# Squares of the gated output, summed step by step in a hybrid decoder layer on one core

## The chip, the core and the metric

The kernel runs on one core of one Trainium2 chip. The metric is the device time of one launch in microseconds (us), as the median of several runs. An engine's name here is that of the profile: PE is TensorE, DVE is VectorE, ACT is ScalarE, POOL is GpSimd, SP is SyncE.

## The reference

One layer over 1024 positions and 1024 channels, in float32. A projection of the normed and modulated input feeds a gated spatial mixer and a Mamba-2 state-space mixer; both go through a projection, are gated, added, projected and added to the input. What the change touches is the end of the state-space mixer: its output `y` of 2048 channels is gated by `silu(z)` and normed by groups of 256 channels.

```python
y_b = ssd_scan(xh, dt, a, bm, cm)                      # chunks of 128 positions
y_b = y_b + xh * d_skip[:, None]
yz = (y_b.reshape(b, s, 2048) * jax.nn.silu(ssm_z)).reshape(b, s, 8, 256)
y_b = rms_norm(yz, ssm_norm_w.reshape(8, -1)).reshape(b, s, 2048)   # yz * rsqrt(mean(yz * yz) + 1e-6) * w
merged = jax.nn.sigmoid(g_a) * (y_a @ w_proj_a) + jax.nn.sigmoid(g_b) * (y_b @ w_proj_b)
```

So for each of 8 groups and each of 1024 positions one sum of 256 squares is needed, and from it one factor.

## The kernel before

The kernel has four parts in time. First the input is normed and transposed. Then, to about 920 us, TensorE multiplies the wide input projection in pairs of 128 columns; other work is hung beside it as tasks. Then comes the **state-space stage**, from about 920 to 1150 us. Last come the products with `w_proj_b` in units named p1, p5, p2, p3, p6, p7 and p4 of eight each, and the output products.

The state-space stage has 32 steps: 8 groups times 4 slices of 256 positions (two chunks of 128). The list `order` runs two groups side by side, so that steps n and n+2 are neighbours of one group. Each step has these parts, for step n:

- `fetch`: SyncE loads `dcy`, the decay row of the step broadcast to all partitions, and then `sl`, the slice with B, C, x and silu(z). There are five buffers of each; the loads stand in SyncE's queue in program order (`pin`), and a load waits until the buffer's last reader is done. For `sl` that is the gating multiply of five steps before.
- `decay`: ACT takes two `ea` (L999) from `dcy`, POOL masks `dcy` in place (L1002), ACT takes eight exponentials of it (L1007).
- `prep`: TensorE makes the products `pc` and transposes `pc` and `px`; DVE makes `xd` and `xe` and multiplies `dcy` (L1027); ACT copies `bn`.
- `front`: TensorE makes `yi` and the state's additions `sp`; POOL and DVE carry the state `st` (L1055, L1057).
- `back`: TensorE makes `yn` from the states. `evacuate` follows: DVE writes `y1` from `yi` and the skip (L1083) and `ym` from `yn` and `ea` (L1087), POOL adds them into `y1` (L1088) and multiplies by the gate into `yz` (L1089). `y1` and `ym` have two buffers each; `yz` holds two steps.

After every second step of a group (`post`), ACT stores `yz`. TensorE's program order is fixed by `pin`: front of step n, some products `pma` of the other branch's projection as filling (`draw`), back of step n, prep of step n+2. Front, back and prep count as one slot each. `later(k, f)` runs f after k more slots. All instructions that are not pinned are put into each engine's queue by a planner that follows expected ready times; on the chip each queue then runs in that order, and an instruction that waits holds up those behind it on its engine.

The sums of squares: five slots after `post`, ACT squares `yz` in place (L1108, it must wait until the store has read it), and POOL adds the two channel halves (L1109). Seventeen slots after `post`, TensorE sums over the partitions with four one-column products per 512 positions (`pq`, the squares as the standing operand), DVE scales them into `ssq` (L1117), positions on partitions, and once per group POOL takes the power −0.5 (L1121). Eight slots on, TensorE transposes the factors (`pr`), DVE copies them (L1131), and ACT stores them to `rs_d`. For the second half of the last two groups the squares go to tiles of their own (L1104), and sums, power and transpose come at the units k = 1, 4 and 6 of p1. The units after the stage load `rs_d` as a broadcast (`rb`) and norm `yz` with it (`y_norm`, L1416).

## Time and profile before

| | us |
|---|---|
| median of 3 runs | 1405.37 |
| lowest and highest run | 1405.05 and 1412.27 |
| the profiled execution: time | 1407.67 |
| the profiled execution: span from first to last instruction | 1405.9 |
| PE busy in the span | 1377.1 (98%) |
| DVE, ACT, POOL busy | 1062.4, 797.0, 213.0 |
| mean granted clock of PE | 0.997 of full |

Times in the profile are microseconds from the span's start. In the timeline a row is: start, length, engine, line, operation, output from inputs, and in brackets how long the engine had been idle and what released it. SPq and ACTq are DMA issues. In a table by windows the figure behind the busy times is the granted clock. In a list of waits a row has the sum, the number and the longest. A matmul in float32 shows as two records.

### The profile page before, as it was taken

How to read it: one execution, taken by the hardware profiler on the slowest of the kernel's cores; microseconds unless marked ns; L12 is line 12 of the kernel's file. 1: busy time of each engine (PE TensorE's matmuls, PEld its weight loads, DVE VectorE, ACT ScalarE, POOL GpSimd, SP SyncE). 2: the span in 40 equal slices, each digit the busy share in tenths (PEclk: the TensorE clock that was granted, in tenths of full speed). 3: DMA queues.
4: the chain of work that ended last, by engine and by line, in shares of the span. 5: the costliest groups of instructions: out<-in, count | busy, mean ns of one | idle time of the engine just before them, and what ended most of it. 6: DMA issues, size and time to landing. Idle time of an engine off the chain costs nothing.

```text
span 1405.9 us, 20633 instructions
## 1 busy us (share of the span) xinstructions
PE 1377.1 (98%) x7035; PEld 1139.9 (81%) x7035; DVE 1062.4 (76%) x1863; ACT 797.0 (57%) x1471; POOL 213.0 (15%) x208
## 2 busy tenths in 40 slices
PE   8999999999999999999999999999999999999997
PEld 6688888888888888888887888888888877878886
DVE  4786776777778889889788796388667767876976
ACT  5764576556656665556565555677766723322443
POOL 0000000000000011111000010038778740000001
PEclk9999999999999999999999999999999999999999
DMA  8653343343344777787675774598778749878903
GB/s 263 173 165 98 113 120 105 105 121 120 116 125 134 214 202 239 236 248 232 192 221 156 240 214 135 173 353 318 262 253 296 275 168 328 320 231 296 350 33 120
DMA packets 273150, 283.37 MB, mean 202 GB/s; under 512 B 15341, under 2 KB 223637, under 8 KB 273045
## 3 DMA queue, kind: packets, MB, share of 16 engines
q1 hardware_dynamic: 185684, 198.52, 44.4%
q10 hardware_dynamic: 87360, 83.54, 17.8%
q8 instruction: 55, 0.90, 0.3%
q14 instruction: 51, 0.41, 0.1%
HBM read 194.55 MB, written 87.46 MB: 201 GB/s over the span
## 4 chain that ended last, share of the span: by engine, by line
PE 80%; DMA 8%; DVE 5%; POOL 2%; issue 2%; ACT 1%; SPq 1%; ACTq 0%; DVEq 0%; POOLq 0%
PE xcb L574 6%; PE xuz L574 6%; PE xz L574 6%; PE xx L574 5%; PE xg L574 5%; PE x L1477 4%; PE yp L1477 4%; PE ox L1676 3%; PE yuz L574 3%; PE ycb L574 3%; PE pma L81 3%; PE xv L574 3%; PE yz L574 3%; PE yg L574 3%; PE yx L574 3%; DMA dcy<-acs_d 3%
## 5 line engine op out<-in xcount | busy, mean ns | idle before, releaser
L793 POOL TENSOR_TENSOR wog<-wog,gb 128x256 f32<-128x256 f32 x16 | 18.3, 1159 | 676.6 <-PE zz L574 413.3
L1007 ACT ACTIVATE dcy<-dcy,nacs 128x128 f32<-128x128 f32 x256 | 78.6, 388 | 14.9 <-POOL dcy L1002 14.5
L1002 POOL TENSOR_SCALAR_AFFINE_SELECT dcy<-dcy 128x1024 f32<-128x1024 f32 x32 | 35.0, 1095 | 135.7 <-ACT ea L999 132.3
L999 ACT ACTIVATE ea<-dcy 64x512 f32<-64x512 f32 x64 | 40.1, 626 | 14.2 <-DMA dcy<-acs_d 13.8
L920 ACT ACTIVATE ac<-ac 128x1024 f32<-128x1024 f32 x32 | 33.9, 1060 | 23.0 <-DVE ac L918 22.8
L81 PE MATMUL pma<-yh,wah 128*128 128x512 f32 x128 | 43.3, 419 | 0.0
L1027 DVE TENSOR_TENSOR dcy<-dcy,pc 128x1024 f32<-128x1024 f32 x32 | 39.0, 1218 | 4.8 <-PE pc L84 3.0
L81 PE MATMUL pma<-yh,wal 128*128 128x512 f32 x128 | 42.5, 413 | 0.0
L1089 POOL TENSOR_TENSOR yz<-y,sl 128x512 f32<-128x512 f32 x32 | 41.4, 1295 | 1.1
L1087 DVE TENSOR_TENSOR ym<-yn,ea 128x512 f32<-128x512 f32 (+1 forms) x32 | 19.9, 622 | 28.5 <-PE yn L81 28.3
L81 PE MATMUL pma<-yl,wah 128*128 128x512 f32 x128 | 40.1, 394 | 0.0
L1088 POOL TENSOR_TENSOR y<-y,ym 128x512 f32<-128x512 f32 (+1 forms) x32 | 36.6, 1144 | 14.4 <-DVE ym L1087 14.4
L81 PEld LDWEIGHTS yn<-sl,st 128*128 128x128 f32 x224 | 30.3, 190 | 8.3 <-issue 4.4
L81 PE MATMUL yn<-sl,st 128*128 128x128 f32 x224 | 31.6, 276 | 4.9 <-DVE st L1057 4.9
L1416 DVE SCALAR_TENSOR_TENSOR yn<-yn,par,rb 128x512 f32<-128x512 f32 x32 | 24.0, 749 | 15.7 <-DMA yn<-yb_d 15.5
L81 PE MATMUL sp<-xe,bn 128*128 128x256 f32 x112 | 32.6, 408 | 3.3 <-DVE ssq L1117 1.7
L81 PE MATMUL yi<-dcy,xd 128*64 128x128 f32 x512 | 35.7, 283 | 0.0
L918 DVE SCALAR_TENSOR_TENSOR ac<-c2x,cwt,ac 128x1023 f32<-128x1023 f32 (+2 forms) x24 | 31.2, 1300 | 5.3 <-ACT ac L916 5.1
L918 DVE SCALAR_TENSOR_TENSOR ac<-c2cb,cwt,ac 128x1023 f32<-128x1023 f32 (+2 forms) x24 | 31.1, 1296 | 4.4 <-ACT ac L916 4.3
L1691 POOL TENSOR_TENSOR r<-r,fnw 128x512 f32<-128x512 f32 x2 | 2.5, 1296 | 203.7 <-DMA out_dram<-r 203.7
L1055 POOL TENSOR_TENSOR st<-st,cd 128x256 f32<-128x256 f32 x48 | 32.1, 668 | 8.0 <-PE yn L81 5.3
L918 DVE SCALAR_TENSOR_TENSOR ac<-c1cb,cwt,ac 128x1023 f32<-128x1023 f32 (+2 forms) x24 | 31.6, 1318 | 1.3 <-ACT ac L916 1.3
(2980 smaller groups left out, 4390.9 us busy)
## 6 DMA issues: line engine op xcount, KB each, us to landing
sl<-s_d SPq DMA_DIRECT2D x32, 768.0 KB
s_d<-ac ACTq DMA_DIRECT2D x32, 512.0 KB
dcy<-acs_d SPq DMA_DIRECT2D x32, 512.0 KB
aw<-in_ada_w_dram SPq DMA_DIRECT2D x16, 512.0 KB
wbr<-in_w_proj_b_dram SPq DMA_DIRECT2D x64, 128.0 KB
wb_d<-wbb ACTq DMA_DIRECT2D x32, 256.0 KB
wb_d<-wbc ACTq DMA_DIRECT2D x32, 256.0 KB
yb_d<-yz ACTq DMA_DIRECT2D x32, 256.0 KB
```

The costliest lines, as they stand in the source:

```text
L81: pin(PE.matmul(acc, l, r, start=first, stop=last))
L574: pin(PE.matmul(ps, lw[:, k * P : (k + 1) * P], r[k], start=first and n + k == 0, stop=n == 2 and k == 3, skip_group_check=not first))
L918: V.scalar_tensor_tensor(ac[:, s:], cc[:, : S - s], conv_wt[:, 3 - s, i : i + 1], ac[:, s:], op0=ALU.mult, op1=ALU.add)
L920: A.activation(ac, ac, AF.Silu)
L999: A.activation(ea[hh * HD : (hh + 1) * HD], dcy.rearrange("p (j e) i l -> p e j (i l)", e=2)[hh * HD : (hh + 1) * HD, hh], AF.Exp)
L1002: G.affine_select(out=d8, in_=d8, compare_op=ALU.is_ge, fill=-1e30, base=0, pattern=[[0, 2 * HPG], [1, P]], channel_multiplier=-1)
L1007: A.activation(dcy[:, h, i, :], dcy[:, h, i, :], AF.Exp, bias=sub[:, i, h : h + 1])
L1027: V.tensor_tensor(d3, d3, pc[:, 0:256].unsqueeze(1).to_broadcast([P, HPG, 256]), op=ALU.mult)
L1088: G.tensor_add(y1[:, :, t0:], y1[:, :, t0:], m[:, :, t0:])
L1089: G.tensor_mul(yz, y1, sl[:, 4:6])
L1477: pin(PE.matmul(ps[j], a[:, v, js], r, start=first and n + k == 0, stop=n == 2 and k == KT - 1, skip_group_check=not first))
L1676: pin(PE.matmul(ps, a[:, tsl], b[:, cs], start=first and n + j == 0, stop=n == 2 and j == 3, skip_group_check=not first))
```

## The change

The squares of each step are taken by themselves. One slot after `evacuate`, ACT squares the step's `yz` into the tile `y1` that held y without its gate, whose content is no longer needed. Two slots later TensorE sums them over the partitions in the other way round: the ones are the standing operand, 32 columns wide, and the squares move, so that each block of 128 positions fills a strip of 32 partitions of the result. The two channel halves are added in PSUM, so POOL's add goes. DVE scales the two strips into a row tile (`cwt`, `tri` or `par`), and after every second step of a group ACT stores one row of each of the four strips to a new tile in memory, `ms_d`. Once per group SyncE loads it back with positions on partitions, POOL takes the power, and ACT stores the factors to `rs_d`; the transposes go. The last two groups do the same at units 1 to 7 after the stage, and their sums no longer come there.

```diff
@@ -55,6 +55,7 @@
 
     acs_d = dt_([NG, 4, HPG, 256], "acs_d")
     rs_d = [dt_([1, S], f"rs_d{g}") for g in range(NG)]
+    ms_d = [dt_([1, S], f"ms_d{g}") for g in range(NG)]
     v_d = dt_([NG, P, NCH * P], "v_d")
     ya_d = [dt_([P, S], f"ya_d{g}") for g in range(NG)]
     mt_d = [dt_([P, S], f"mt_d{g}") for g in range(NG)]
@@ -1087,52 +1088,51 @@
             V.tensor_tensor(m[:, :, t0:], yn.rearrange("p (j l) -> p j l", j=2)[:, :, t0:], ea[:, :, t0:], op=ALU.mult)
             G.tensor_add(y1[:, :, t0:], y1[:, :, t0:], m[:, :, t0:])
             G.tensor_mul(yz, y1, sl[:, 4:6])
+            later(1, self.square, s, yz, y1)
 
         def post(self, q):
 
             g = self.g
             for j in range(2):
                 store(yb_d[2 * g + j][:, q * 512 : (q + 1) * 512], self.yz[q][:, j])
-            yz = self.yz[q]
-            if g < NG - 2 or q == 0:
-                later(5, self.squares, yz, [yz[:, j] for j in range(2)])
-                later(17, self.post2, q, [yz[:, 0]])
-            else:
-                self.late = [turn(r, f"sq{g}", F32) for r in (y1_r, ym_r)]
-                with tc.high_priority():
-                    for j in range(2):
-                        A.activation(self.late[j], yz[:, j], AF.Square)
-
-        def squares(self, yz, sq):
+
+        def square(self, s, yz, y1):
+
+            A.activation(y1, yz, AF.Square)
+            later(2, self.post2, s, y1)
+
+        def post2(self, s, sq):
+
+            g, b = self.g, 2 * (s % 2)
+            pq = bank(f"pq{g}_{s}")
             for j in range(2):
-                A.activation(sq[j], yz[:, j], AF.Square)
-            G.tensor_add(sq[0], sq[0], sq[1])
-
-        def post2(self, q, sq):
-            g = self.g
-            pq = rows_bank[0](f"pq{g}_{q}")
-            for i in range(4):
-                for j, t in enumerate(sq):
-                    mm(pq[:, i : i + 1], t[:, i * P : (i + 1) * P], ones[:, 0:1], j == 0, j == len(sq) - 1)
-            V.tensor_scalar(ssq[:, g * NCH + q * 4 : g * NCH + q * 4 + 4], pq[:, 0:4], 1.0 / 256, EPS,
-                            op0=ALU.mult, op1=ALU.add)
-            if q == 1:
-                c8 = slice(g * NCH, (g + 1) * NCH)
-                G.tensor_tensor(ssq[:, c8], ssq[:, c8], nhalf, op=ALU.pow)
-                if g < NG - 2:
-                    later(8, self.post3)
+                for i in range(2):
+                    mm(pq[32 * (b + i) : 32 * (b + i) + 32, 0:P], ones[:, 0:32], sq[:, j, i * P : (i + 1) * P],
+                       j == 0, j == 1)
+            row = (cwt, tri, par)[(g + s // 2 * 2) % 3]
+            half = slice(32 * b, 32 * b + 64)
+            V.tensor_scalar(row[half, :], pq[half, 0:P], 1.0 / 256, EPS, op0=ALU.mult, op1=ALU.add)
+            if s % 2:
+                store(ms_d[g][:, s // 2 * 512 : s // 2 * 512 + 512].rearrange("o (i p) -> (o i) p", p=P),
+                      row[0:P:32, :])
+            if s == 3 and g < NG - 2:
+                for n, f in ((6, self.post3), (12, self.post4), (15, self.post5)):
+                    later(n, f)
 
         def post3(self):
 
-            g = self.g
-            pr = rows_bank[0](f"pr{g}")
-            tp(pr[0:NCH, 0:P], ssq[:, g * NCH : (g + 1) * NCH], ident)
-            row = (cwt, tri)[g % 2][0:NCH, :]
-            V.tensor_copy(row, pr[0:NCH, 0:P])
-            store(rs_d[g].rearrange("o (c p) -> (o c) p", p=P), row)
+            load(ssq[:, self.g * NCH : (self.g + 1) * NCH], ms_d[self.g].rearrange("o (p c) -> (o p) c", p=P))
+
+        def post4(self):
+
+            c8 = ssq[:, self.g * NCH : (self.g + 1) * NCH]
+            pin(G.tensor_tensor(c8, c8, nhalf, op=ALU.pow))
+
+        def post5(self):
+
+            store(rs_d[self.g].rearrange("o (p c) -> (o p) c", p=P), ssq[:, self.g * NCH : (self.g + 1) * NCH])
 
     groups = [Group(g) for g in range(NG)]
-    rows_bank = [bank]
 
     order = [(2 * r + j, s) for r in range(NG // 2) for s in range(4) for j in range(2)]
     done_f, done_d = [0], [0]
@@ -1590,12 +1590,13 @@
     BESIDE = [(j // 2, wo_load, ("b11", j)) for j in range(4)] + [(2 + j, wo_load, ("t1", j)) for j in range(4)]
     BESIDE += [(2 + j, wo_split, ("b11", j)) for j in range(4)]
     BESIDE += [(3 + j, row_load, (j,)) for j in range(5)] + [(j + 4, split, ("s1", j - 1)) for j in (1, 3)]
+    late_todo = {1: groups[NG - 2].post3, 4: groups[NG - 2].post4, 5: groups[NG - 2].post5,
+                 3: groups[NG - 1].post3, 6: groups[NG - 1].post4, 7: groups[NG - 1].post5}
     for u, (nm, k) in enumerate(units):
         if k == 0:
             if nm == "p1":
                 psy = banks("yp5", "y")
                 psx = banks("x", "x")
-                rows_bank[0] = lambda name: psy[("pr6", "pr7", "pq6_1", "pq7_1").index(name)]
             elif nm in ("p2", "p3"):
                 psy = banks(f"y{nm}", "y")
             elif nm == "p6":
@@ -1603,14 +1604,10 @@
             ps = psy if nm in ("p2", "p5", "p3") else psx
         multiply(u, ps)
         ahead(u)
-        if nm == "p1" and k in (1, 4):
-            late = groups[NG - 2 + k // 4]
-            late.post2(1, late.late)
         if nm == "p1" and k == 4:
             for tags, _ in (y1_r, ym_r):
                 room.extend(tags)
-        if nm == "p1" and k in (4, 6):
-            groups[NG - 4 + k // 2].post3()
+        late_todo.get(u, lambda: None)()
         if k % 2 and nm in GATES:
             gate_load(GATES[nm][0] + k // 2, GATES[nm][1])
         if nm == "p4":
```

## The prediction

> **What bounds the kernel now.** I read the page first, then the stage that the change touches, by windows and by engine, then its waits, its chain, and the order in which the build lays each engine's instructions.

> ```profile
> PE 1377.1 (98%) x7035; PEld 1139.9 (81%) x7035; DVE 1062.4 (76%) x1863; ACT 797.0 (57%) x1471; POOL 213.0 (15%) x208
> ```
> ```profile
> 952.07:1147.25 195.18, 186.57 (x1410) 162.60 (x1411) 141.13 (x262) 126.32 (x327) 153.30 (x148) 0.99 0.74 256
> ```

> TensorE is busy for 98% of the span, so the kernel is as long as TensorE's work plus its gaps. The second row is the stretch of the state-space steps (columns: length; busy time of PE, PEld, DVE, ACT, POOL; granted clock; DMA share; GB/s), from the start of the gating multiply of step 2 to the end of that of step 31. I number the 32 steps 0 to 31 as the order written out in the kernel has them. From start to start, 29 steps take 195.18 − 1.28 = 193.9 us, 6.69 us each. TensorE is idle for 8.6 us (195.18 − 186.57) in all; POOL, DVE and ACT have room. Whoever makes TensorE wait in each step sets a new pace; whoever merely frees another engine gains 8.6 us at most.

> How close the other queues come to that is seen in the waits and in one loop of the timeline (start, length, engine, line).

> ```profile
> ACT ea L999 <- DMA dcy<-acs_d: 13.8, 11, 3.4
> ACT yz L1108 <- DMA yb_d<-yz: 9.5, 9, 2.9
> ```
> ```profile
> 1005.30 1.28 POOL L1089 TENSOR_TENSOR yz<-y,sl 128x512 f32<-128x512 f32 x1
> 1006.61 0.32 SPq L90 DMA_DIRECT2D sl<-s_d  x1
> ...
> 1009.18 0.45 SPq L90 DMA_DIRECT2D dcy<-acs_d  x1
> 1010.19 2.45 ACT L1007 ACTIVATE dcy<-dcy,nacs 128x128 f32<-128x128 f32 x8 [1.20 <-POOL dcy L1002]
> ...
> 1017.75 1.27 ACT L999 ACTIVATE ea<-dcy 64x512 f32<-64x512 f32 x2 [1.01 <-DMA dcy<-acs_d]
> 1018.04 1.28 POOL L1088 TENSOR_TENSOR y<-y,ym 128x512 f32<-128x512 f32 x1
> 1019.84 1.10 POOL L1002 TENSOR_SCALAR_AFFINE_SELECT dcy<-dcy 128x1024 f32<-128x1024 f32 x1
> 1020.91 1.29 POOL L1089 TENSOR_TENSOR yz<-y,sl 128x512 f32<-128x512 f32 x1
> ```

> The multiply `yz` of step 10 ends at 1006.58. It was the last reader of a slice of s_d, so SyncE issues the load of `sl` for step 15 at 1006.61, and behind it, in queue order, the decay row `dcy` of step 16 at 1009.18 (four loads of weights and gates stand between here). The row lands, ACT takes `ea` from it (1017.75, it had waited for this DMA), POOL masks it (1019.84), and behind the mask stands `yz` of step 12 (1020.91). So today a multiply hangs on the multiply **two** steps earlier, by way of a DMA. Without loads in between:

> ```profile
> 1094.04 0.32 SPq L90 DMA_DIRECT2D sl<-s_d  x1
> 1094.47 0.66 SPq L90 DMA_DIRECT2D dcy<-acs_d  x1
> ...
> 1101.11 1.27 ACT L999 ACTIVATE ea<-dcy 64x512 f32<-64x512 f32 x2 [0.61 <-DMA dcy<-acs_d]
> 1102.45 1.09 POOL L1002 TENSOR_SCALAR_AFFINE_SELECT dcy<-dcy 128x1024 f32<-128x1024 f32 x1 [0.61 <-ACT ea L999]
> ```

> Summed: 0.03 to the issue of `sl`, 0.43 to that of `dcy`, 6.64 from there to `ea`, 1.27 for `ea`, 0.07 to the mask, 1.07 from the mask's start to the multiply's, 1.29 for the multiply: **10.8 us per loop**. Over two steps that is 5.4 per step, under the 6.69 that TensorE needs. It is hidden, with little to spare.

> **What the change does to this.** It takes the 14 adds of squares off POOL and squares each step by itself into the tile `y1`, so ACT no longer waits for the store of yz:

> ```profile
> L1108 ACT ACTIVATE yz<-yz x28: 612/632/635, 959.0 to 1126.6; 128x512 f32<-128x512 f32 x28
> L1109 POOL TENSOR_TENSOR yz<-yz x14: 1268/1286/1302, 964.3 to 1129.8; 128x512 f32<-128x512 f32 x14
> ```

> That is 14 × 1.286 = 18.0 us of POOL and the 9.5 us of ACT's waits above. Neither ends on TensorE (the second row's gaps bound the gain), so by itself it gains next to nothing. What counts is the order that results. The build orders each engine's queue by what it expects to be ready first, and POOL, with less to do, now takes masks earlier (mask, `ea` and `exp` carry the number of the step that they prepare; `sq` is the square, `pq` its sums, `tp` the transposes):

> ```
> GpSimd, before: yz10 sel15 st y11 st yz11 pow st add y12 st sel16 yz12 pow st y13 sel17 yz13
> GpSimd, after:  yz10 st pow y11 st sel16 yz11 st pow y12 st sel17 yz12 st y13 sel18 yz13
> ScalarE, after: sq10 ms ea16 rs bn exp16 yb sq11 ms ea17 rs bn exp17 sq12 wah ea18 bn exp18 sq13
> TensorE, after: yn11 tp13 yi12 sp12 pq11 pma yn12 tp14 yi13 sp13 pq12 pma yn13
> SyncE, both:    sl16 dcy17 sl17 dcy18 sl18
> ```

> Before, `yz` of step 12 stands behind the mask of step 16, four ahead, whose row was issued behind yz 10. After, it stands behind the mask of step 17, five ahead, and that row is issued behind `sl` of step 16, which waits for yz 11. The same 10.8 us loop now closes over **one** step. This holds for steps 3 to 7, 10 to 15, 18 to 23 and 26: 18 links. In steps 8, 9, 16, 17, 24 and 25 no such mask stands ahead, and after 26 none is left.

> Before, that would have hurt only POOL, since `pq` came 17 slots after its pair of steps. Now `pq` of a step comes two slots after its square is asked for, right behind the next step's `yi` and `sp`. TensorE takes it in order, so it waits for POOL's multiply and ACT's square, and behind it wait all the filling products `pma`, `yn`, and through them the next step. The square in turn stands behind `exp` of five steps ahead.

> **The sum.** First TensorE's own loop, whether it is longer than the DMA's:

> ```profile
> 1068.20 1.86 PE pma L81 x8
> 1070.06 0.89 PE yn L81 x8
> 1072.06 0.79 PE pq L81 x8
> 1072.84 1.02 PE yi L81 x16
> 1073.87 1.06 PE sp L81 x4
> 1074.93 2.29 PE pma L81 x10
> ```
> ```profile
> 1008.01 0.69 DVE L1087 TENSOR_TENSOR ym<-yn,ea 128x512 f32<-128x512 f32 x1 [0.86 <-PE yn L81]
> ```

> I count from the end of a multiply. `exp` of 2.45 starts 0.04 after the mask's end (1010.15 to 1010.19) and so ends 1.22 after the multiply; then come the square 0.63, a handover 0.05, `pq`, `pma` 1.86 or 2.29 (2.08), `yn` 0.89, `ym` 0.05 + 0.69, `y` 0.07 + 1.28, the mask 1.07 and the multiply 1.29. The new `pq` is four pairs of records with 32 columns and 128 rows. No such form is in this stage; `yi` with 64 columns takes 1.02/16 = 0.064 us a record, `yn` with 128 columns 0.89/8 = 0.111, so eight lie between 0.51 and 0.89. Less than 0.51 is possible if four strips overlap better than two, to nothing at the least. I take 0.51, the nearest form. Sum: 1.22 + 0.63 + 0.05 + 0.51 + 2.08 + 0.89 + 0.74 + 1.35 + 1.07 + 1.29 = **9.8 us**. So the DMA's 10.8 ends last, with 1.0 us between them. TensorE's own work in a step is transposes 1.11 (1072.06 − 1070.95), yi 1.02, sp 1.06, pma 2.08, yn 0.89, pq 0.51 = 6.7; it stands still for 4.1.

> - 18 links: 18 × (10.8 − 6.69) = +74.0.
> - The three pairs without a mask: the first step has TensorE's loop less the mask (9.8 − 1.07 = 8.75), the second has no `exp` ahead of its square either (7.5): 3 × (16.25 − 13.38) = +8.6.
> - Steps 27 to 31: 8.75 + 4 × 7.5 − 5 × 6.69 = +5.3.
> - SyncE's four extra loads lie ahead of `dcy` for steps 10, 16, 21 and 26; three of these (links 5, 11 and 21) close a loop. They cost 2.57 (1006.61 to 1009.18) against 0.43: 3 × 2.14 = +6.4. Before, two steps' length covered them.
> - The first `pq` follows both first `yn` without a step between: its chain (0.74 + 1.35 + 1.29 + 0.63 + 0.1 = 4.1) less the 1.1 of transposes ahead of it: about +2.9, an estimate. The last one: 4.1 less a `pq` (0.51) and a `pma` of eight (1.86): +1.7.
> - In the next stage the two late sums go: 32 records at 0.79/8 (3.2 us) and the wait for their power, below: −7.0, at the least −3.2, if another wait is ready to take its place.

> ```profile
>   POOL ssq L1121: 3.8, 2
> ```

> Together +91.9. The 13 sums that went from inside the stage (0.79 each) and the 32 new ones don't enter, since TensorE waits there anyway.

> **Edits at nothing.** The moments' sixteen stores and eight loads and the factors' eight stores through memory: each is an issue of the size of the SPq rows above (0.32 to 0.45 us) on ACT or SyncE. ACT blocks on the moments' store until `pq` and the DVE row are done, 1 us or so after the square, while the row for the next `ea` is in flight for 6.64: covered. On SyncE they delay a `dcy` by one issue in links 10, 18 and 26 (1.2 us in all, within the rounding). The power (POOL, before y) lies in POOL's wait for `ym`. The last two groups' factors are stored at the sixth and eighth unit of the products after the stage and read at the fifteenth:

> ```profile
> L1477 PE MATMUL yp<-p5bh,p5a x64: 389/389/389, 1186.1 to 1207.6; 128*128 128x512 f32 x64
> ```

> Eight units take 21.6 us, so nine leave 24 us for two small transfers. If that cover were gone, one transfer (6.64) would be paid.

> The profiled execution took 1407.67 us (span 1405.9), 2.3 above the median of the runs shown. 1407.67 + 91.9 = 1499.6, and on the median's footing **1497**.

> **Bounds of the landing.** The 6.64 is the disputed cost:

> ```profile
> 1049.59 0.36 SPq L90 DMA_DIRECT2D dcy<-acs_d  x1
> ...
> 1055.20 1.28 ACT L999 ACTIVATE ea<-dcy 64x512 f32<-64x512 f32 x2 [0.66 <-DMA dcy<-acs_d]
> ```

> 5.61 here, where `sl` was far ahead; 8.57 in the loop above (1009.18 to 1017.75), behind four loads. I take 6.64, because it has exactly one `sl` 0.43 ahead, as every link will have. With 5.61 the DMA's loop would be 9.77 and TensorE's sets the pace: 18 × 1.0 less, 1479. With 8.57 in all links: 1532.

> **The clock.** A gap of TensorE has a second price here:

> ```profile
> 1030.49 0.68 PE L81 MATMUL yn<-sl,st 128*128 128x128 f32 x4 [2.77 <-DVE st L1057]
> ```
> ```profile
> 1028.00:1030.00 2.00, 0.00 (x0) 1.00 0.00 0
> 1030.00:1032.00 2.00, 1.51 (x10) 0.81 0.75 187
> 1032.00:1034.00 2.00, 2.00 (x15) 0.50 1.00 409
> 1034.00:1036.00 2.00, 2.00 (x17) 0.83 0.17 65
> ```

> After the one gap of 2.77 us the granted clock (third figure) is 0.81, 0.50, 0.83 over 2 us each: 0.76 + 2.0 + 0.68 = 3.4 us at half. Each link will have a gap of 4.1. A stretch of 3.4 at half adds 1.7 to TensorE's loop, of which 1.0 is covered: +0.7 for each link, 1510 if all have it. [...]

> **The rivals.**
> - *Half clock in most links.* If everything between a gap and the next `yn` (0.51 + 2.08 + 0.89 = 3.5) runs at half, TensorE's loop is 13.3 and sets the pace: 18 × 2.5 more, 1542; with one stretch each, 1510. Middle 1526. For: the row of 0.50. [...] Chance 0.2.
> - *A shorter loop.* Rows land sooner because a slower stage moves fewer bytes per us; then TensorE's loop rules, 1479, and if the square isn't held by `exp` (1.22 less) and SyncE's loads hide, 18 × 2.2 + 6.4 less: 1451. For: a DMA share of 0.74 now. Against: `sl` and `dcy` still go together. Chance 0.14.
> - *Only the unmasked loop.* Were masks and `exp` never late, the 7.5 of above would hold in all steps: 29 × 0.81 − 2.4 = +21, 1426. Against: the orders. Chance 0.03.
> - *Faster.* TensorE meets `pq` 3.2 after `yn` (1.11 + 1.02 + 1.06). If the chain to the square, 0.74 + 1.35 + 1.29 + 0.63 + 0.1 = 4.1 without a mask, is really under 3.2, and the masks aren't late, `pq` never waits. For: the legend of the page calls spans on POOL rough, and 2.6 of the 4.1 are POOL's. Then the stage's 8.6 us of gaps and the 7.0 of the late sums go, against 32 × 0.51 − 13 × 0.79 = 6.1 more products: 1396. Against: the links' masks, and no landing shown under 5.6. Chance 0.04.
> - *No change.* A chain just above 3.2 gives back what the gaps and late sums free: 1405. Chance 0.03.
> - The forecast: 0.56.

> **How the numbers follow.** Slower is 0.56 + 0.2 + 0.14 + 0.03 = 0.93, same 0.03, faster 0.04; 0.5% is 7 us, about what a measurement of this kernel can tell. The range goes from the short loop's end, 1451, to the half clock's, 1542: it leaves out the three last rivals, 0.1, and what of the first two lies beyond their ends.

> **What will show it.** Right: the eight-in-ten busy digits of PE drop to six or seven over the stage only; PE's longest wait is `pq` on ACT's square, some 60 to 80 us; yz starts 10 to 11 us apart in the links and less in steps 8, 9, 16, 17; `ea` waits for `dcy<-acs_d` in nearly every step; the clock shows 0.5 stretches. Wrong: PE stays above 95% in the stage, or `yz` steps of under 8 us in the links, or rows landing within 3 us.

## The result and the profile after

| | before | after |
|---|---|---|
| median of the runs, us | 1405.94 (6 runs, 1402.67 to 1412.27) | 1549.28 (6 runs, 1547.03 to 1554.82) |
| ratio, 95% interval | | 1.1022 [1.1002, 1.1042] |
| span of the profiled execution, us | 1405.9 | 1547.8 |
| from the start of yz 2 to the start of yz 31, us | 193.9 | 324.3 |
| time of PE at half clock, without the stretch at the very end of each (8.1 and 8.4), us | 3.4 (1 stretch) | 126.3 (24 stretches) |

Slower by 10.2%, as to sign and place as forecast, and 52 us more than 1497; the range ended 7 us below. From here on line numbers are those of the changed kernel, in the steps one above the old ones; an experiment's own edit shifts them again. The page of the changed kernel, with its totals, PE's busy tenths and its granted clock in 40 slices:

```profile
PE 1429.8 (92%) x7139; PEld 1163.4 (75%) x7139; DVE 1065.5 (69%) x1871; ACT 797.4 (52%) x1471; POOL 194.0 (13%) x194
...
PE   8999999999999999999999998686766788999997
...
PEclk9999999999999999999999999787887978999999
```

PE has lost its nines in the state-space stage and just behind it, and nearly the same slices have lost clock. The stage by windows, from the start of yz 2 to the end of yz 31 (before, the same row had 195.18 us, 186.57 of them busy, at clock 0.99):

```profile
960.40:1286.00 325.60, 234.71 (x1527) 183.24 (x1525) 145.29 (x271) 123.27 (x315) 133.88 (x133) 0.83 0.44 152
```

PE now idles for 325.60 − 234.71 = 90.9 us, before for 8.6, and is busy for 48.1 us longer. Two costs, then: standing still (+82.3) and more busy time (+48.1). Of the second, 8.7 us are more work; the rest, as the first experiment shows, is the same work at a slower clock. The waits in the stage say for what (sum, times, longest):

```profile
PE pq L82 <- ACT y L1101: 94.5, 29, 6.1
DVE ym L1088 <- PE yn L82: 72.1, 25, 5.2
ACT ea L1000 <- DMA dcy<-acs_d: 47.7, 13, 8.9
ACT ea L1000 <- DVE ym L1088: 46.3, 11, 7.5
...
ACT y L1101 <- POOL yz L1090: 25.0, 8, 9.2
```

In 29 of 32 steps TensorE stands before `pq` until ACT has squared. One link in the timeline, in a choice of its rows:

```profile
1088.97 1.27 POOL L1090 TENSOR_TENSOR yz<-y,sl 128x512 f32<-128x512 f32 x1
1089.04 2.44 ACT L1008 ACTIVATE dcy<-dcy,nacs 128x128 f32<-128x128 f32 x8 [0.64 <-POOL dcy L1003]
...
1091.39 0.61 ACT L1101 ACTIVATE y<-yz 128x512 f32<-128x512 f32 x1
1092.05 1.07 PE L82 MATMUL pq<-y,ones 128*32 128x128 f32 x8 [3.49 <-ACT y L1101]
...
1093.05 1.22 PE L82 MATMUL pma<-yh,wal 128*128 128x512 f32 x2
...
1096.63 1.58 PE L82 MATMUL yn<-sl,st 128*128 128x128 f32 x8
...
1098.24 0.69 DVE L1088 TENSOR_TENSOR ym<-yn,ea 128x512 f32<-128x512 f32 x1 [4.79 <-PE yn L82]
...
1098.97 1.27 ACT L1000 ACTIVATE ea<-dcy 64x512 f32<-64x512 f32 x2 [6.97 <-DVE ym L1088]
1099.02 1.28 POOL L1089 TENSOR_TENSOR y<-y,ym 128x512 f32<-128x512 f32 x1 [0.63 <-DVE ym L1088]
...
1100.31 1.09 POOL L1003 TENSOR_SCALAR_AFFINE_SELECT dcy<-dcy 128x1024 f32<-128x1024 f32 x1
...
1101.37 1.27 POOL L1090 TENSOR_TENSOR yz<-y,sl 128x512 f32<-128x512 f32 x1
```

The loop from multiply to multiply takes 12.40 us (1088.97 to 1101.37), and it is TensorE's, item by item as the prediction listed it: exps, square, `pq`, `pma`, `yn`, `ym`, `y`, mask, multiply. Two things differ. `ea` has to be taken from `dcy` before the mask may overwrite it, and it waits in this loop not for its rows but for `ym`: there are five `ea` buffers, and the `ea` of five steps on overwrites the one that `ym` has just read. And `pq`, `pma` and `yn` take 1.07, 3.6 and 1.58 us, not 0.63, 1.9 and 1.05 as in the first experiment below, where the clock is full. The granted clock (third figure from the end) tells why, over windows of 3.41 us:

```profile
1084.07:1087.48 3.41, 3.41 (x34) 3.10 (x34) 2.15 (x4) 0.90 (x2) 1.48 (x2) 1.00 0.01 2
1087.48:1090.90 3.42, 1.08 (x12) 0.51 (x6) 2.82 (x6) 2.59 (x9) 2.74 (x3) 1.00 0.00 0
1090.90:1094.31 3.41, 2.26 (x11) 1.63 (x12) 0.28 (x1) 1.10 (x3) 0.00 (x0) 0.50 0.86 293
1094.31:1097.72 3.41, 3.41 (x12) 2.85 (x12) 0.00 (x0) 0.00 (x0) 0.00 (x0) 0.50 0.24 96
1097.72:1101.14 3.42, 3.24 (x32) 2.50 (x31) 2.70 (x4) 1.63 (x3) 2.72 (x3) 1.00 0.00 0
```

PE stands in the second window; in the third and fourth, just when `pq` to `yn` hold everything up, it runs at half. So the wait costs a second time.

The other links, read the same way: in 13 of the 18, `y` was finished when `ea` was or after it, so the mask waited for TensorE's loop; in the other five (5, 11, 18, 21 and 26) `ea` was last and had waited for its rows.

### The profile page after: what moved, and what is told of

Its sections match the earlier page's. It is cut to its first block, busy times and chain, and to the rows that moved or that the text cites. A ratio compares the mean times of both kernels' runs of the same rounds, so it can differ in the third digit from the quotient of the medians.

```text
span 1547.8 us, 20942 instructions
## 1 busy us (share of the span) xinstructions
PE 1429.8 (92%) x7139; PEld 1163.4 (75%) x7139; DVE 1065.5 (69%) x1871; ACT 797.4 (52%) x1471; POOL 194.0 (13%) x194
## 4 chain that ended last, share of the span: by engine, by line
PE 73%; DMA 7%; DVE 5%; ACT 5%; POOL 4%; issue 4%; SPq 1%; ACTq 0%; POOLq 0%; DVEq 0%
PE x L1477 6%; PE xuz L575 5%; PE pma L82 5%; PE xcb L575 5%; PE xz L575 5%; PE xx L575 5%; PE xg L575 4%; PE yp L1477 3%; PE ox L1673 3%; PE yuz L575 3%; PE xv L575 3%; PE ycb L575 3%; DMA dcy<-acs_d 2%; PE yx L575 2%; PE yg L575 2%
## 5 line engine op out<-in xcount | busy, mean ns | idle before, releaser
L82 PE MATMUL pq<-y,ones 128*32 128x128 f32 x256 | 27.1, 349 | 94.6 <-ACT y L1101 94.5
L82 PEld LDWEIGHTS pq<-y,ones 128*32 128x32 f32 x256 | 14.6, 133 | 108.0 <-ACT y L1101 106.7
L1008 ACT ACTIVATE dcy<-dcy,nacs 128x128 f32<-128x128 f32 x256 | 78.3, 388 | 23.9 <-POOL dcy L1003 23.6
L1088 DVE TENSOR_TENSOR ym<-yn,ea 128x512 f32<-128x512 f32 (+1 forms) x32 | 19.9, 623 | 72.1 <-PE yn L82 72.1
L82 PE MATMUL pma<-yh,wah 128*128 128x512 f32 x128 | 53.8, 510 | 0.0
L82 PE MATMUL pma<-yh,wal 128*128 128x512 f32 x128 | 53.1, 504 | 0.0
L82 PE MATMUL pma<-yl,wah 128*128 128x512 f32 x128 | 51.1, 489 | 0.0
L1089 POOL TENSOR_TENSOR y<-y,ym 128x512 f32<-128x512 f32 (+1 forms) x32 | 37.7, 1177 | 34.8 <-DVE ym L1088 34.8
L82 PEld LDWEIGHTS pma<-yh,wal 128*128 128x128 f32 x128 | 30.3, 249 | 11.0 <-issue 4.7
L82 PEld LDWEIGHTS pma<-yl,wah 128*128 128x128 f32 x128 | 31.6, 247 | 8.2
L82 PEld LDWEIGHTS pma<-yh,wah 128*128 128x128 f32 x128 | 29.5, 244 | 10.5 <-issue 4.7
L82 PEld LDWEIGHTS yn<-sl,st 128*128 128x128 f32 x224 | 34.1, 213 | 4.1 <-issue 0.5
L1101 ACT ACTIVATE y<-yz 128x512 f32<-128x512 f32 x32 | 19.9, 620 | 29.3 <-POOL yz L1090 25.0
```

The lines of the kernel that those rows point to most:

```text
L82: pin(PE.matmul(acc, l, r, start=first, stop=last))
L1008: A.activation(dcy[:, h, i, :], dcy[:, h, i, :], AF.Exp, bias=sub[:, i, h : h + 1])
L1089: G.tensor_add(y1[:, :, t0:], y1[:, :, t0:], m[:, :, t0:])
```

## The experiments

The theory now: TensorE waits for the square in each step; the work behind that wait runs at half clock and leads back to the next square. The rivals: the loop through the rows (multiply, SyncE's load, landing, `ea`, mask), which the prediction took for the pace, sets it; or the new instructions cost by themselves. The first four kernels ran beside the kernel before at 1405.31 us.

### The sums further back

```diff
-            later(2, self.post2, s, y1)
+            later(5, self.post2, s, y1)
```

> The sums of a step's squares come 5 slots after the square instead of 2, so on TensorE's queue they stand behind the front of the step after next. Theory (TensorE's wait in order for the square is what costs): the chain from yn to the square has a whole step more, the waits of pq on ACT's square fall from 94 us to under 15, the clock stays full, and the time comes to 1395 to 1420 us. First rival (the DMA loop of my forecast sets the pace whatever TensorE does): the multiplies stay over 10 us apart in the steps whose mask is five ahead, 1480 to 1510. Second rival (the new strip products, rows and trips through memory cost by themselves): 1530 or more, since all of them are still there.

Measured: 1411.58 us, ratio 1.0045 [1.003, 1.006]. One number gives back 137.7 of the 143 us, with every new instruction still there. The stage by windows, and the longest of PE's waits in it:

```profile
953.44:1150.78 197.34, 195.28 (x1540) 156.46 (x1538) 149.19 (x272) 125.06 (x324) 134.47 (x134) 1.00 0.73 251
```
```profile
PE pq L82 <- DVE xe L1024: 1.4, 3, 0.7
```

No wait for a square is left. The same work, but for 13 records, kept PE busy for 234.71 us in the changed kernel and for 195.28 here: **some 39 us were the half clock**, and the idle time fell from 90.9 to 2.1. The new instructions are not the cost; what they add to TensorE's work in the stage is 8.7 us (195.28 against 186.57), of which the old idle time takes up most. The rows aren't yet acquitted: with less waiting the planner also put most masks only four steps ahead, so their loop was gone too. That is taken up below.

### Work into the gap

```diff
+            for _ in range(12):
+                mm(pq[:, P : 2 * P], ident, ones)
```

> The changed kernel with 12 products of identity and ones (128x128, no use made of them) on TensorE ahead of each step's sums, in the time in which it waits for the square: about 2.7 us more work per step, 85 us in all. Theory (half clock after each gap is a good part of the loss): the granted clock stays at 1.0, a step with the mask five ahead goes from 12.3 to about 10.1 us, and the time falls to about 1500 in spite of the added work. DMA loop: such a step goes to 10.8 at most, 1515. If the clock has no part: 1549 if the work fits the gaps, up to 1630 if it doesn't.

Measured: 1526.94 us, 1.0866 [1.0849, 1.0882]. The changed kernel with 12 products more in each step is 22 us *faster*. Half clock fell from 126.3 to 20.5 us, but the 18 links only from 12.29 to 11.55 in the mean, not to 10.1: the size was missed. The test is not quite clean, since the planner also moved the mask out of two links, 5 and 21. Waits in the stage:

```profile
ACT ea L1000 <- DMA dcy<-acs_d: 51.8, 12, 9.0
...
PE pq L82 <- ACT y L1101: 28.9, 19, 4.5
ACT ea L1000 <- DVE ym L1088: 28.0, 9, 6.4
```

With TensorE near full speed, `ea` waits for the rows longer than for `ym` (51.8 us against 28.0): the other loop stands close behind.

### The order written out

ACT's and POOL's main instructions of the stage are pinned: the masks of four steps on come behind the multiply, the square comes ahead of the exps. The sums stay two slots behind. Of the edit, two places:

```diff
-            G.tensor_mul(yz, y1, sl[:, 4:6])
+            pin(G.tensor_mul(yz, y1, sl[:, 4:6]))
...
-        decays(n + 4)
+        decays(n + 5)
```

> The changed kernel with squares, decays, masks and gating multiplies pinned in an order by hand: the mask four ahead behind the multiply, and the square ahead of the eight exponentials. The sums stay two slots behind the square. Theory: the loop is only yn, ym, y, yz, square, pq, pma, 7.5 us a step, with gaps of about 1 us that don't bring the clock down: 1420 to 1440. If the place of the sums alone were the cost and the order had no part: 1520 or more. If the new instructions cost by themselves: 1530 or more.

Measured: 1506.23 us, 1.0729 [1.0699, 1.0759]. A miss by some 70 us: the order is under a third of the 143. Neither mask nor exps stand in the loop now, the 18 links fell to 10.28 us, and yet PE waits, and the clock falls after a gap of 2.3 us, as in these two windows of 3.41 us:

```profile
PE pq L82 <- ACT y L1101: 63.8, 30, 5.0
```
```profile
1060.22:1063.63 3.41, 1.15 (x12) 0.85 (x12) 1.62 (x5) 2.00 (x5) 2.52 (x3) 1.00 0.27 49
1063.63:1067.05 3.42, 3.42 (x10) 2.65 (x9) 0.69 (x1) 2.18 (x7) 0.00 (x0) 0.50 0.83 335
```

### A sixth buffer for `ea`

```diff
-            if n < 2:
+            m = (nstep[0] - 1) % 6
+            if m < 2:
...
+            elif m == 5:
+                ea = p2x.tile([P, 2, 256], F32, name=f"ea{nm}", tag="ex", bufs=1)
```

(`xd` has two buffers in place of three, for room.)

> The changed kernel with six buffers of ea instead of five (and two of xd instead of three), so that ea of five steps ahead need not wait for this step's ym, which reads the buffer that it overwrites. Queue order as in the changed kernel, masks five ahead. Theory (the loop runs through this buffer: pq, pma, yn, ym, ea, mask, exponentials, square): ACT's waits of ea on ym go, the step falls from 12.3 to the DMA loop's 10.8 or so, 1515 to 1530 us. Rival (the DMA loop sets the pace already, the buffer only looks like it): no change, 1545 to 1555.

Measured: 1559.66 us, 1.1104 [1.1083, 1.1126], no gain at all and slower than either forecast. The waits for `ym` are gone, and the rows took their place:

```profile
PE pq L82 <- ACT y L1104: 98.7, 30, 7.1
ACT ea L1003 <- DMA dcy<-acs_d: 75.5, 18, 8.9
```

The test is not a clean one, though. The planner's order moved too, and in many steps the mask came to stand ahead of y's add, so that the add joined the loop through the rows:

```profile
1089.99 1.09 POOL L1006 TENSOR_SCALAR_AFFINE_SELECT dcy<-dcy 128x1024 f32<-128x1024 f32 x1
1091.05 1.28 POOL L1092 TENSOR_TENSOR y<-y,ym 128x512 f32<-128x512 f32 x1
1092.41 1.27 POOL L1093 TENSOR_TENSOR yz<-y,sl 128x512 f32<-128x512 f32 x1
```

From multiply to multiply it is 11.23 us here (1081.18 to 1092.41). What it shows is that the buffer alone is not the bound: where it doesn't hold `ea`, the rows do.

### No square

The next four ran beside the kernel before at 1405.82.

```diff
-            A.activation(y1, yz, AF.Square)
```

> Leaves out the 32 squarings on ScalarE: the strips sum y itself instead of its square. Every other instruction stays, and the queues nearly as they were; TensorE's sums then wait for GpSimd's add of y and its gating multiply alone (the tile is read only, so the sums need the add, 2.0 us ahead of the multiply's end and 4.4 to 5.0 ahead of the square's end with its place behind the exps). Theory (TensorE's in-order wait for the square closes a loop through sums, next yn, ym, ea, mask, exps, square, and its gaps bring the half clock): the loop loses mask, multiply, exps and square, what is left of it is about 5 to 6 us, shorter than the 6.7 that the step needs: 1400 to 1420, less than 15 us of half clock. Rival A (the DMA loop from the multiply over the five-ahead load to the next mask sets 10 to 11 us by itself): 1470 to 1510, since that loop is untouched. Rival B (both loops are needed, each covers the other): 1410 to 1470.

Measured: 1410.51 us, 1.0033 [1.0019, 1.0046], half clock 3.4 us. `pq` now needs only POOL's add, and waits for next to nothing:

```profile
PE pq L82 <- POOL y L1089: 1.1, 3, 0.6
```

As the theory had it. But the expectation was wrong that the loop through the rows stays untouched: as in the first experiment the planner moved most masks to four ahead once nothing was late.

### The written order, with work in the gap

The written order as above, and:

```diff
+            for _ in range(8):
+                mm(pq[:, P : 2 * P], ident, ones)
```

> The ordered kernel of e3_order with 8 dummy products of 128x128 ahead of each step's sums (about 1.9 us of work that needs nothing), into a spare part of the same bank. It tells apart, in e3_order, the wait from the clock: there the link took 10.3 us with gaps of 2 to 2.3 us and 75 us of half clock. If the half clock that the gaps bring is most of what e3_order still costs (theory): the gaps shrink to under 1 us, the half clock falls below 25 us, and the step to 8.5 to 9.5 us although 60 us of work are added: 1465 to 1490, faster than the 1506 without the dummies. Rival (the wait itself, at any clock, is what costs; the clock only looks bad): the dummies fill the gap and nothing is gained, 1500 to 1515.

Measured: 1479.45 us, 1.0523 [1.0499, 1.0546]. Inside the forecast, 27 us faster than the written order without the dummies. The stage of the written order without and with them:

```profile
962.48:1245.02 282.54, 223.86 (x1525) 176.67 (x1524) 149.84 (x272) 126.39 (x326) 135.69 (x134) 0.89 0.52 175
```
```profile
963.41:1222.34 258.93, 245.21 (x1988) 210.94 (x1987) 145.16 (x271) 125.76 (x325) 134.70 (x134) 1.00 0.56 190
```

Some 50 us of work were added (245.21 against 195.28 in the first experiment, without them and at clock 1.00), half clock went from 75.1 to 3.4 us, and the stage got 23.6 us shorter. Here the order was written out in both, so the clock is what differs: filling the wait with useless work cost less here than the wait with the slower clock behind it (258.93 us against 282.54).

### One slot

```diff
-            later(2, self.post2, s, y1)
+            later(3, self.post2, s, y1)
```

> The changed kernel with one number different: the sums come three items behind the square in the planner's list, not two. On TensorE's queue they then stand right behind the next step's yn, where before they stood ahead of the 8 to 10 products of the projection and that yn. Theory (what costs is that the sums gate the next yn, through it the next multiply and square): a square that is late then holds up only work of the step after, the loop spans two steps, and half of it is 5 to 6.5 us: 1408 to 1425, little half clock. Rival A (any wait for the square on TensorE brings gaps and so the half clock, the place only shifts them): 1470 to 1530. Rival B (distance must cover the whole way from yn to the square, 9 to 10 us, so that three items are not enough while five are): 1440 to 1480.

Measured: 1424.42 us, 1.014 [1.0104, 1.0177]. `pq` moves from ahead of the filling products and `yn` to behind `yn`, and 125 of the 143 us come back:

```profile
PE pq L82 <- ACT y L1101: 10.1, 6, 2.1
```

A late square no longer delays the `yn` that the next square needs, only work of the step after, and the prediction's loop of 9.8 us, now spread over two steps, is less than TensorE's own work in them (13.4). That is argued from the sum; here too the planner put the masks only four ahead, so the run does not show the place of the sums by itself. The slot also gives the square the 3 us of `pma` and `yn` more; the run doesn't separate the two. Five slots, the whole way from `yn` to the square, weren't needed.

### Half the sums on DVE

The sums five slots behind, and ahead of them DVE adds the two halves of the squares, so that TensorE needs two products in place of four.

```diff
+            V.tensor_add(y1[:, 0], y1[:, 0], y1[:, 1])
...
-            for j in range(2):
-                for i in range(2):
-                    mm(..., ones[:, 0:32], sq[:, j, i * P : (i + 1) * P], j == 0, j == 1)
+            for i in range(2):
+                mm(..., ones[:, 0:32], sq[:, 0, i * P : (i + 1) * P])
```

> A try at a kernel that beats both: the sums five items behind the square (as e1_sums_later, ratio 1.0045), and between them VectorE adds the two halves of each square (one operation of 128x256 more a step, 32 in all, about 0.3 to 0.4 us each), so that TensorE sums two strips a step and not four products: 0.31 us less on TensorE in each step. In e1_sums_later TensorE was 99% busy in the stage (197.9 of 200 us) against 95% before, so TensorE's time should set the stage: 32 x 0.31 = 10 us less there, stage 196 to 188-193, the whole 1400 to 1408. Rival: the stage is set by the DMA loop and the masks, not by TensorE (before's stage had 4.7% idle on TensorE and was no longer than this): 1408 to 1412, no gain.

Measured: 1412.57 us, 1.0053 [1.0033, 1.0073]: no gain, as the rival had it, if 0.6 us beyond its end. The group of DVE's new adds and the stage by windows:

```profile
L1106 DVE TENSOR_TENSOR y<-y 128x256 f32<-128x256 f32 x28 | 16.9, 602 | 3.1 <-ACT y L1101 2.7
```
```profile
955.00:1145.00 190.00, 183.35 (x1364) 145.47 (x1363) 157.98 (x290) 123.83 (x322) 131.29 (x129) 0.98 0.75 256
```

An add took 0.60 us, not 0.3 to 0.4. PE has 6.7 us of idle time again in these 190 us, and the stage from yz 2 to yz 31 takes 199.0, not less than 196.1: at about this length the stage has other limits than TensorE's work, which ones was not separated.

### The loop through the rows by itself

This takes the prediction's own loop: the sums five slots behind, ACT's and POOL's main instructions pinned, and the mask of five steps on forced between y's add and its multiply in 25 steps, its row loaded just ahead. The other kernels of this group ran beside 1405.01.

```diff
+            if 2 <= turn_no[0] < len(order) - 5:
+                at = order[turn_no[0] + 5]
+                groups[at[0]].rows(at[1])
+                decays(turn_no[0] + 6)
             pin(G.tensor_mul(yz, y1, sl[:, 4:6]))
...
-            later(2, self.post2, s, y1)
+            later(5, self.post2, s, y1)
```

(Of the edit, the main part. `rows` is the part of `fetch` that loads `dcy`; the load of `sl` stays where it was.)

> The sums five items behind the square, so that TensorE waits for no square, and the order on GpSimd and ScalarE written out so that in each of 25 steps the mask of five steps on stands between y's add and its gating multiply (its row load issued just ahead of it, the load of the tile with the gate still behind the multiply). It keeps the loop that the prediction summed to 10.8 us (multiply, SyncE's next load, rows landing, ea, mask, multiply) and takes away TensorE's. Theory (the loop through the rows is real wherever this order stands, the changed kernel only had a second loop of about the same length that ran at half clock): 25 steps at 10.3 to 11.3 us, the whole 1490 to 1525; ScalarE's wait for the rows the longest. Rival (that loop is no bound, the rows land ahead of need once TensorE is free): 1408 to 1425.

Measured: 1519.16 us, 1.0813 [1.0796, 1.0831]. The loop is real. One of its turns, from one issue of `sl` to the next, and waits of the stage:

```profile
1085.75 0.32 SPq L91 DMA_DIRECT2D sl<-s_d  x1
1086.17 0.37 SPq L91 DMA_DIRECT2D dcy<-acs_d  x1
...
1091.27 1.27 ACT L1006 ACTIVATE ea<-dcy 64x512 f32<-64x512 f32 x2 [3.52 <-DMA dcy<-acs_d]
...
1092.61 1.09 POOL L1009 TENSOR_SCALAR_AFFINE_SELECT dcy<-dcy 128x1024 f32<-128x1024 f32 x1 [5.67 <-ACT ea L1006]
1093.67 1.29 POOL L1100 TENSOR_TENSOR yz<-y,sl 128x512 f32<-128x512 f32 x1
...
1094.99 0.32 SPq L91 DMA_DIRECT2D sl<-s_d  x1
```
```profile
PEld pq L82 <- ACT y L1111: 81.3, 25, 6.0
ACT ea L1006 <- DMA dcy<-acs_d: 73.4, 19, 6.2
...
PE pq L82 <- ACT y L1111: 71.3, 25, 5.6
```

This turn takes 9.24 us, with 5.10 from the issue of `dcy` to `ea`, and is one of the shortest. The 18 links took 11.2 us in the mean, and without the three that have SyncE's extra loads (5, 11 and 21) 10.66, with 6.21 from the issue to `ea`; the prediction had 10.8 and 6.64. So by itself the loop was summed about right. The expectation that TensorE would wait for no square was wrong: with the multiplies that far apart it catches up with the square even five slots behind, 71.3 us in all, with 102.4 us of half clock. But that sets no pace here: in each of the 18 links `y` was finished at least 4.3 us before `ea` was.

### Both loops out, trips doubled, and the order alone

The written order together with the sums five slots behind:

> The written order of e3_order (mask four ahead, behind the multiply, the square ahead of the exps) together with sums five items behind the square, the two things that each took out a loop. Theory: neither loop is left, TensorE's time sets the stage as in e1_sums_later: 1404 to 1412. Try for a kernel no slower than the one before; the rival is that a written order takes away what the planner gains by moving around (e3_order's first links, 15.5 and 12.3 us, were longer than any of the others): 1412 to 1430.

Measured: 1409.79 us, 1.0039 [1.0025, 1.0053]; links of 6.88, the stage 194.5 us. Close to before, not below it. With this run the two loops can be told apart by kernels in which masks, exponentials, squares and multiplies are all pinned, so that the planner cannot move them:

| written order | sums two slots behind | sums five slots behind |
|---|---|---|
| mask four ahead, behind the multiply | 1506.23 | 1409.79 |
| mask five ahead, ahead of the multiply | not run | 1519.16 |

TensorE's wait alone costs 96 us, the loop through the rows alone 109, and the changed kernel, with both, 143 above the kernel before. The two run beside each other and do not add up; neither alone is the whole.

The first experiment with every transfer of the way through memory made twice:

```diff
             load(ssq[...], ms_d[self.g].rearrange("o (p c) -> (o p) c", p=P))
+            load(ssq[...], ms_d[self.g].rearrange("o (p c) -> (o p) c", p=P))
```

(The stores to `ms_d` and `rs_d` likewise.)

> e1_sums_later with every transfer of the way through memory made twice (16 stores of sums, 8 loads of 128x8, 8 stores of factors more). The prediction took this way at nothing, since y_load wants the factors stages later. Theory: within 3 us of e1_sums_later (1408.5 to 1414.5). Rival: small transfers with many short pieces hold up SyncE's queue or the DMA queues and with them the row loads, one microsecond or two each: 1425 to 1445.

Measured: 1422.37 us, 1.0131 [1.0113, 1.0148], 10.8 more than with single trips: the expectation failed, and so did the doubling as a measure. Of SyncE's own waits from 925 to 1180 us these have to do with the trips:

```profile
SPq L91 <- DMA ssq<-ms_d: 30.6, 6, 7.5
SPq L91 <- DMA rs_d<-ssq: 7.7, 3, 4.0
```

The second load writes where the first writes, so SyncE's queue waits for the first to land, some 5 us each, with the row loads behind it. With single trips neither wait is among SyncE's. So the doubled trips have a cost that single ones don't have; that the 10.8 us are this wait is likely, but not shown. What single trips can cost in the stage is bounded by the first experiment, where TensorE idles for 2.1 us in all.

The kernel before with the written order, as a try at a faster version:

> The kernel before, with its ea, masks, exps and gating multiplies in the written order (mask four ahead behind the multiply), its own sums and squares unchanged. A try at a version faster than both: before's stage left TensorE 4.6% idle (181.4 of 190 us busy), some of it behind steps where the planner put a mask five ahead of the multiply (10.2 us between two multiplies, the longest). If those are removable: stage 193.9 to 187-191, 1400 to 1404. Rival (TensorE's idle time there comes from other waits, and the written order is as good as the planner's): 1404 to 1409.

Measured beside 1406.33: 1408.55 us, 1.0012 [0.9997, 1.0026]. PE's idle time in the stage stays (181.81 of 190 us busy). No version beat the kernel before.

## Why the prediction was wrong

Its terms against the two profiled executions, in us:

| term | forecast | measured |
|---|---|---|
| start, up to yz 2 | +2.9 | +8.3 |
| 18 links, with SyncE's extra loads | +80.4 | +100.9 |
| three pairs without a mask | +8.6 | +13.0 |
| steps 27 to 31 | +5.3 | +16.6 |
| after the last multiply | −5.3 | +3.1 |
| sum | +91.9 | +141.8 |

**Right:** the sign; the mechanism, that the sums two slots behind the square make TensorE stand in nearly every step, shown with the order fixed (1506.23 against 1409.79) and, with masks that moved too, by later sums (1411.58 and 1424.42) and without the square (1410.51); the loop through the rows (10.8 forecast, 10.66 alone); the order of the queues with the mask five steps ahead, in just the 18 links named; SyncE's extra loads: links 5, 11 and 21 took 13.9, 14.3 and 13.8 us, 2.05 above the mean of the other fifteen (11.95), forecast 2.14, and in all three `ea` waited for its rows. The memory trips and the DVE rows at nothing are borne out within the 2.1 us above.

**Right by luck in part:** the time that TensorE stands still. The forecast's stage of 288.2 us (193.9 + 94.3) less 29 times TensorE's 6.7 leaves 94 us, and 90.9 were measured; but it was worked out from the loop through the rows, which ended last in five of the 18 links.

**The step that failed** is the price of the clock: "a stretch of 3.4 at half adds 1.7 to TensorE's loop, of which 1.0 is covered: +0.7 for each link", left out of the sum. Its cover was "the DMA's 10.8 ends last, with 1.0 us between them". In the link shown above `ea` waits for `ym`, not for the rows: TensorE's loop ended last, as in 13 of the 18, so its half clock counted in full. `pq`, `pma` and `yn` took 6.2 us in place of 3.5, and the loop of 9.8 became 12.4. Nor did the half clock fall into the idle time, where it would have cost nothing: in the link shown PE works 5.67 of the 6.82 us at half (2.26 and 3.41), right behind the window with the gap, and that is when the products run that everything waits for. A stretch was also longer than taken: 13 of the 24 were of 6.83 us. In the link shown its first window still holds 1.15 us of the gap; in the five traces of the last section a window at half with more than 1.0 us idle was followed by another one at half 31 times of 31. By PE's busy time the half clock cost the stage some 39 us of TensorE's time, where the sum for the stage was short by 36.1.

The other 13.8 of the 49.9 us lie at the start (+5.4) and behind the last multiply (+8.4). At the start a stretch of 3.4 us at half follows the first gap, of 3.5 us. Behind the last multiply there are 10.2 us at half and a wait of 4.1 us for `tha` of the other branch (1.4 before), taken at nothing. There the prediction also misread a row: the "3.8, 2" of the power is one wait seen twice, 1.7 us of PE and 2.1 us of PEld at the same product, so at most 1.7 could be saved. How the 8.4 divides among these is open.

The second way to the mask, by which `ym` frees the buffer of the next `ea`, was not seen at all. By itself it cost next to nothing (in that link `ea` ends at 1100.24, `y` at 1100.30, and the mask starts behind both at 1100.31), but it ties `ea` to TensorE's loop however soon the rows land.

**The rival** *half clock in most links* (0.2) is what happened, 7 us above its end of 1542. That its number came so near is partly luck: it was priced for the links alone, 45 us over the forecast, and the links took only 20.5 us more than forecast. Pairs, last steps, start and end took 29.5 more, and these have gaps and half clock too, with no mask of five steps on ahead. *A shorter loop* expected rows to land sooner, as they did by 0.4 us with the loop by itself (6.21), but the loop that TensorE then sets has the clock in it. *No change* and *faster* rested on a chain of 3 to 4 us before `pq`; TensorE waited up to 6.1.

**What was to show it:** PE's digits fell to six, seven and eight in the stage; PE's longest wait was `pq` on the square, 94.5 us against 60 to 80; the multiplies stood 12.3 us apart, not 10 to 11, and 9.0 and 7.1 in steps 8 and 9, but 14.3 in step 17; half-clock stretches came. `ea` waited for the rows only 13 times and 11 times for `ym`: the sign, beside the sizes, that did not fit the pace the prediction had chosen.

## What to carry to other kernels

Where an engine takes its queue in order, ask of a wait what stands behind it: a consumer placed ahead of work on which its own next producer depends turns a delay into a loop, and one slot further back, behind that work, the same consumer cost 1.4% instead of 10.2%, with masks that the planner had moved too. Price a gap of TensorE at its length and, where the trace shows a slower clock behind gaps, at that too (here 90.9 us of idle time and some 39 us of half clock), and don't count that as covered by a second loop that is only 10% longer on paper. When two loops are about equal, taking a piece of one away shows nothing (a sixth buffer: 1559.66), and the planner's order moves with each edit, so write the order out before testing either loop by itself.

## What the runs showed of the clock

| idle in a window at full clock | next window at half |
|---|---|
| under 1.6 us | 0 of 273 |
| 1.6 to 1.8 us | 3 of 8 |
| 1.8 to 2.0 us | 20 of 22 |
| 2.0 us and more | 68 of 68 |

From a window at half, the next was at full 89 times of 89 with under 0.5 us idle, once of 7 with 0.5 to 1.0, and never of 31 with more. So in these five traces a window at full clock with 1.8 us or more of idle time was followed by one at half 88 times of 90, and the full clock came back 89 times of 89 behind a window at half with under 0.5 us idle, but once of 38 behind one with more. The rows above show the clock fall after windows with 1.08, 1.15 and, at the edge, about 1.7 us of work in them.
